# Block copies of the transposed norm and feed-forward blocks moved to SBUF-to-SBUF transfers, and x split for two tiles at once

## The chip, the cores and the metric

The kernel runs on one core of a Trainium2 chip. The metric is the device time of one execution in microseconds (us), the median of three runs. Engines: PE (TensorE, matmuls; PEld its weight loads), DVE (VectorE), ACT (ScalarE), POOL (GpSimd) and SP (SyncE, which here only issues DMAs). Each engine works through its own instructions in order.

## The reference

A trunk of two residual layers over 256 tokens of width 2048, all in float32. Layer 0 mixes tokens by grouped-query attention, layer 1 by a recurrent block (projection, convolution, two gated scans, output projection); each is followed by a SwiGLU feed-forward block of width 5632.

```python
for i in range(DEPTH):
    h = rms_norm(x, norm_mix[i])
    if i % N_MIXERS == 0:
        mix = attention_mixer(h, attn_w_qkv[j], ...)
    else:
        mix = recurrent_mixer(h, rnn_w_in[j], ...)
    x = x + mix
    x = x + swiglu(rms_norm(x, norm_ffn[i]), ffn_w_gate[i], ffn_w_up[i], ffn_w_down[i])

def rms_norm(x, g):
    y = xf * lax.rsqrt(jnp.mean(xf * xf, axis=-1, keepdims=True) + EPS)
    return y * g

def swiglu(h, w_gate, w_up, w_down):
    return (jax.nn.silu(h @ w_gate) * (h @ w_up)) @ w_down
```

## The kernel before

**Split matmuls.** Every matmul operand is a pair: hi, a rounded copy (made by ACT), and lo, the remainder (made by DVE as raw minus hi). A product is three matmuls: hi by hi, lo by hi, hi by lo. Weights stream from HBM in loads of 512 KB, issued by SP into eight buffers named raw (L140 in `load_half`, L157 in `load_seven`). `load_half` makes one cast (L145) and one remainder (L146) of a load. `load_seven` takes a pair of loads (gate and up) and makes the operands of a seven-product scheme: combinations of blocks on DVE (L169, the first of them by an accumulating DMA of POOL, L176, or on DVE, L174), casts L163 and L170 (its first is called ohi), remainders L164 and L171 (olo, lo). PE's order is the order of the code; the other engines' order is set by a scheduler from its own model of time, except where `follow` and `behind` chain instructions: `behind("cast", ...)` and `behind("rest", ...)` keep ACT's casts and DVE's remainders in the order of the code.

**x.** The residual stream `x_tm` lies with tokens on partitions (128 x 2 x 2048). A norm (class `Norm`) needs it with features on partitions. As soon as a group of 512 columns of x is final, `Norm.add(g)` squares it for the mean (L444) and calls `turn(g, engines)`: `turn_blocks` transposes 32 x 32 blocks in one DVE instruction (L408, tile two or x into one), and 16 copies of 32 partitions x 256 columns (L416, one into two) put the blocks where a 128-wide transpose would have them. The engines given in the call share the copies: ACT and POOL for groups 0 to 2, DVE, ACT and POOL for group 3. `scale` then makes the pair of each of the four tiles: ACT scales by the gain (L435), DVE takes the remainder (L436). For the feed-forward norm `form` makes four more operands per pair of tiles (ACT scale L466, four POOL instructions L472, cast L474, remainder L475: tiles form, fh, fl). The tiles one and two exist once each.

**Feed-forward units.** `ffn` runs 11 units of 512 hidden features per layer. In a unit, PE goes over eight pairs of tiles of x: those listed in SEVEN (or FEWER for the first three units) take 21 matmuls of 512 columns for two loads, the others 24. The unit's end combines the accumulators on DVE (L770 to L773, L791, L794, L795), with SiLU on ACT, into h (tile two). h is turned like x: one transpose, 16 copies, and then `whole` makes the split pair act (cast L801, remainder L802). Units 1 to 9 spread this over the next unit: the list `tail` holds four pieces of four copies each, the last one with `whole`, and every `load_seven` takes one piece. All copies of units 0 to 9 are ACT's; unit 0 does them in one piece at once, and unit 10 shares them between ACT and DVE. Between the units stand the down products, drained by ACT (L818) and added to x by accumulating DMAs of POOL.

**The recurrent layer's norm.** After the feed-forward block of layer 0 the norm of layer 1 is turned the same way, group 3 last. `Norm.spread` (L492, L493) makes the row of token factors: dg on DVE, and two small matmuls of PE that stand between those of the first projection.

Of the kernel before, what the change touches and what calls it, by code (L numbers as in the profile page):

```python
# [12 lines left out]
F32 = mybir.dt.float32  # L13
# [5 lines left out]
P = 128  # L19
# [55 lines left out]
def trunk(ctx, tc, w, out):  # L75
# [242 lines left out]
    def block(xs, k, a):  # L318
        return tuple(xs[k][:, s + a * P : s + (a + 1) * P] for s in (0, S))
# [85 lines left out]
    def turn_blocks(src, engines, own=None, spread=None):  # L405
        turned = tmp("one", (P, 2, WIDE), bufs=1)
        own = tmp("two", (P, 2, WIDE), bufs=1) if own is None else own
        dve.transpose(turned, src)  # L408
        t = own.rearrange("p a (b c) -> p (a b) c", c=S)

        def move(i):
            of = turned[32 * i : 32 * i + 32].rearrange("p a (k j c) -> p k a j c", k=4, j=4)
            for j in range(4):
                to = t[32 * j : 32 * j + 32].rearrange("p k (a i c) -> p k a i c", a=2, i=4)
                eng = engines[(4 * i + j) % len(engines)]
                m = (eng.copy if eng is act else eng.tensor_copy)(to[:, :, :, i, :], of[:, :, :, j, :])  # L416
                if spread is not None:
                    behind("cast", m)

        for i in range(4):  # L420
            move(i) if spread is None else spread.append(partial(move, i))
        return t

    class Norm:
# [5 lines left out]

        def scale(self, src):
            k = len(self.xs)
            g = col(self.g[0], self.g[1] + k)
            t = xp.tile([P, 2 * S], F32R, tag="xg", name=nm("xg"), bufs=16)
            newest["xh"] = act.activation(t[:, :S], src, AF.Copy, scale=g)  # L435
            newest["xl"] = dve.scalar_tensor_tensor(  # L436
                t[:, S:], src, g, t[:, :S].bitcast(F32), ALU.mult, ALU.subtract
            )
            self.xs.append(t)
# [6 lines left out]
        def add(self, g):  # L446
# [4 lines left out]
            self.turn(g, (act, pool) if g < NW - 1 else (dve, act, dve, pool))  # L451
# [3 lines left out]
        def turn(self, g, engines):  # L455
            t = turn_blocks(x_tm[:, :, g * WIDE : (g + 1) * WIDE], engines)
            for k in range(4):
                self.scale(t[:, k, :])
            for i in range(2):
                if self.g[0] == "norm_ffn" and 2 * g + i in SEVEN:  # L460
                    self.form(2 * g + i, t[:, 2 * i : 2 * i + 2, :])

        def form(self, c, src):
            v, t = (tmp("form", (P, 2 * S)).rearrange("p (a b) -> p a b", a=n) for n in (2, 4))
            for j in range(2):
                act.activation(v[:, j, :], src[:, j, :], AF.Copy, scale=col(self.g[0], self.g[1] + 2 * c + j))  # L466
# [283 lines left out]
    def ffn(norm, nxt):  # L750
# [3 lines left out]
        def unit(seven, beside, engines, soon):  # L754
# [42 lines left out]
            t, ht = act_four(), turn_blocks(h, engines, h, tail if beside else None)  # L797

            def whole(move=list):
                move()  # L800
                act.copy(t[:, :, :S], ht)  # L801
                dve.tensor_tensor(t[:, :, S:], ht, t[:, :, :S].bitcast(F32), ALU.subtract)  # L802

            if beside:
                tail.append(partial(whole, tail.pop()))
            else:
                whole()
            return [t[:, k, :] for k in range(UNIT)]
# [3 lines left out]
        for what, i in ffn_plan():  # L812
            if what == "unit":
                hid[int(np.searchsorted(ends, i, "right"))] += unit(FEWER.get(i, SEVEN), 0 < i < ends[-1] - 1, (act,) if i < ends[-1] - 1 else (act, dve), i < ends[0])
# [228 lines left out]
```

## Time and profile before

| | |
|---|---|
| median of 3 runs | 1953.04 us (1952.99 to 1953.76) |
| the profiled execution | 1952.89 us, span 1951.1 us |
| granted TensorE clock | 1.000 |
| PE busy | 1938.0 us of the span, 9224 matmuls |
| DVE, ACT, POOL busy | 1768.6, 1448.3, 401.3 us |
| DMA | 426 MB, q1 (SP) 58.0% and q0 (POOL) 11.9% of 16 engines' span |

How to read the rows: in the timeline a row is the start, the duration, the engine, the line, the operation, out<-in, the shape and the count; in brackets stands the idle time of the engine before it and who ended it. Matmuls are pipelined and a row's duration overlaps the next, so the distance between starts tells how fast PE goes. A row of a stretch has its length, each engine's busy time with the number of instructions, the granted clock, and the DMA share. A group's row has busy time and mean ns after the first bar, idle time before them after the second. A row of DMA issues ends with the median time from issue to landing.

### The profile page before, as it was taken

To read this page: it belongs to the slowest core of one execution; us is meant where nothing else is said; L and a number is where in the kernel's file an instruction comes from. 1 tells how busy PE (TensorE), PEld (TensorE's weight loads), DVE (VectorE), ACT (ScalarE), POOL (GpSimd) and SP (SyncE) were. 2 spreads that over 40 slices of the span, in tenths; PEclk is the share of its full clock that TensorE was granted. 3 is DMA by queue.
4 is the path that set the end of the run, shared out by engine and by line. 5 is a ranking of instruction groups with operands and counts; after the bars stand their busy time and mean duration, and the time that the engine had idled before them with its cause. 6 is when DMAs were issued, how large, how long until landed. Compare 5 with 4: busy or idle time off the path is not lost.

```text
span 1951.1 us, 27630 instructions
## 1 busy us (share of the span) xinstructions
PE 1938.0 (99%) x9224; PEld 1624.0 (83%) x9224; DVE 1768.6 (91%) x2417; ACT 1448.3 (74%) x2358; POOL 401.3 (21%) x497
## 2 busy tenths in 40 slices
PE   9999999999999999999999999999999999999999
PEld 8898888788888888888899998887888888888887
DVE  7878698999999999998799997898999999999993
ACT  7677686777777777777698887866778776787772
POOL 0442250011101111010465450520101111011100
PEclk9999999999999999999999999999999999999999
DMA  8434746698878978787365556555878888788872
GB/s 328 156 127 152 248 158 197 196 272 236 248 233 243 262 240 246 235 244 246 126 223 188 189 164 245 175 194 174 253 236 248 245 248 253 231 246 251 246 257 86
DMA packets 131727, 426.42 MB, mean 219 GB/s; under 512 B 14720, under 2 KB 14976, under 8 KB 131584
## 3 DMA queue, kind: packets, MB, share of 16 engines
q1 hardware_dynamic: 108944, 383.21, 58.0%
q0 software_dynamic: 22496, 41.43, 11.9%
q8 instruction: 72, 1.18, 0.2%
q14 instruction: 71, 0.58, 0.1%
q10 hardware_dynamic: 144, 0.02, 0.0%
HBM read 382.13 MB, written 2.10 MB: 197 GB/s over the span
## 4 chain that ended last, share of the span: by engine, by line
PE 92%; DVE 4%; ACT 1%; issue 1%; DMA 1%; POOL 0%; SPq 0%; ACTq 0%; DVEq 0%; POOLq 0%
PE acc L326 14%; PE acc L323 14%; PE acc L324 14%; PE pm L326 11%; PE pm L323 11%; PE pm L324 11%; PE acc L294 8%; PE acc L292 4%; PE pm L306 1%; PE pm L307 1%; PE pm L305 1%; DVE lo L146 1%; ACT hi L145 1%; DVE lo L164 0%; DMA raw<-in_w_in_dram 0%
## 5 line engine op out<-in xcount | busy, mean ns | idle before, releaser
L146 DVE TENSOR_TENSOR lo<-raw,hi 128x1024 fp32r<-128x1024 f32 (+1 forms) x474 | 574.5, 1240 | 77.1 <-ACT hi L145 75.3
L145 ACT CAST hi<-raw 128x1024 fp32r<-128x1024 f32 (+1 forms) x474 | 478.4, 1045 | 116.5 <-PE acc L324 72.1
L326 PE MATMUL acc<-lo,xg 128*128 128x512 f32 x744 | 290.9, 391 | 2.0 <-DVE lo L146 1.8
L323 PE MATMUL acc<-hi,xg 128*128 128x512 f32 x744 | 290.0, 390 | 0.0
L324 PE MATMUL acc<-hi,xg 128*128 128x512 f32 x744 | 289.6, 389 | 0.0
L164 DVE TENSOR_TENSOR lo<-raw,hi 128x1024 fp32r<-128x1024 f32 x232 | 275.0, 1217 | 6.5 <-ACT hi L163 3.8
L294 PE MATMUL acc<-xg,hi 128*128 128x512 f32 x832 | 271.7, 397 | 0.6 <-ACT hi L145 0.6
L163 ACT CAST hi<-raw 128x1024 fp32r<-128x1024 f32 x232 | 234.6, 1048 | 41.0 <-issue 14.4
L176 POOL DMA_DIRECT2D raw<-raw x90 | 77.7, 863 | 903.9 <-DVE raw L174 369.5
L323 PE MATMUL pm<-hi,act 128*128 128x512 f32 x512 | 199.2, 389 | 0.0
L324 PE MATMUL pm<-hi,act 128*128 128x512 f32 x512 | 199.2, 389 | 0.0
L326 PE MATMUL pm<-lo,act 128*128 128x512 f32 x512 | 199.2, 389 | 0.0
L416 ACT COPY two<-one 32x256 f32<-32x256 f32 x420 | 169.7, 404 | 24.7 <-DVE one L408 16.5
L292 PEld LDWEIGHTS acc<-xg,lo 128*128 128x128 f32 x832 | 156.3, 188 | 35.4 <-DVE lo L146 2.8
L323 PE MATMUL acc<-hi,act 128*128 128x512 f32 x448 | 174.9, 390 | 0.4 <-DVE two L794 0.4
L326 PE MATMUL acc<-lo,act 128*128 128x512 f32 x448 | 174.4, 389 | 0.0
L324 PE MATMUL acc<-hi,act 128*128 128x512 f32 x448 | 174.4, 389 | 0.0
L292 PE MATMUL acc<-xg,lo 128*128 128x256 f32 x832 | 171.8, 281 | 1.2 <-DVE lo L146 1.2
L326 PEld LDWEIGHTS acc<-lo,xg 128*128 128x128 f32 x744 | 139.7, 188 | 34.1 <-DVE lo L146 5.4
L324 PEld LDWEIGHTS acc<-hi,xg 128*128 128x128 f32 x744 | 139.7, 188 | 29.2
L323 PEld LDWEIGHTS acc<-hi,xg 128*128 128x128 f32 x744 | 139.7, 188 | 28.6
L170 ACT CAST hi<-raw 128x512 fp32r<-128x512 f32 x232 | 137.1, 622 | 32.8 <-DVE raw L169 31.8
(221 smaller groups left out, 3852.1 us busy)
## 6 DMA issues: line engine op xcount, KB each, us to landing
raw<-in_w_gate_dram SPq DMA_DIRECT2D x176, 512.0 KB, 4.6
raw<-in_w_up_dram SPq DMA_DIRECT2D x176, 512.0 KB, 5.5
raw<-in_w_down_dram SPq DMA_DIRECT2D x176, 512.0 KB, 4.4
raw<-in_w_in_dram SPq DMA_DIRECT2D x64, 512.0 KB, 4.4
raw<-raw POOLq DMA_DIRECT2D x90, 256.0 KB, 5.8
raw<-in_w_q_dram SPq DMA_DIRECT2D x32, 512.0 KB, 3.8
raw<-in_w_o_dram SPq DMA_DIRECT2D x32, 512.0 KB, 4.2
x<-form POOLq DMA_DIRECT2D x64, 256.0 KB, 6.7
```

The costliest lines, as they stand in the source:

```text
L145: behind("cast", act.copy(hi[:, sl], raw[:, sl]))
L146: behind("rest", dve.tensor_tensor(lo[:, sl], raw[:, sl], hi[:, sl].bitcast(F32), ALU.subtract))
L163: behind("cast", act.copy(hi, src))
L164: behind("rest", dve.tensor_tensor(lo, src, hi[:].bitcast(F32), ALU.subtract))
L170: behind("cast", act.copy(hi, o))
L176: pool.dma_start(out=t1, in_=b11, accum_op=ALU.add)
L292: pe.matmul(acc[:, S:], w, xs[k][:, :S], start=False, stop=stop)
L294: pe.matmul(acc, w, xs[k], start=(k == 0), stop=stop)
L323: pe.matmul(o, xh, wh, start=start, stop=False)
L324: pe.matmul(o, xl, wh, start=False, stop=False)
L326: pe.matmul(o, xh, wl, start=False, stop=stop)
L416: m = (eng.copy if eng is act else eng.tensor_copy)(to[:, :, :, i, :], of[:, :, :, j, :])
```

## The change

`turn_blocks` becomes `move_blocks`. The transpose is made in two halves (one per half of the tokens, 512 columns each, reading and writing in strides), so that each of the 16 moves is 32 partitions x 256 columns in one piece. If no engines are given, the 16 moves are DMAs from SBUF to SBUF issued by SP. This holds for all turns of the norms except group 3 of the recurrent layer's (still DVE, ACT and POOL), and for units 0 to 9 of each feed-forward block; unit 10 keeps ACT and DVE. Unit 0 now also defers `whole`; it stands behind the third `load_seven` of the next unit. `Norm.scaled` treats two tiles at once: two scales of ACT into v (tile form), one cast of both (xg, hi), one remainder of both on DVE; `form` takes v from it. The tiles xg and act hold their pairs in another layout, which `block` knows.

```diff
     def block(xs, k, a):
+        if isinstance(xs[k], tuple):
+            t, n = xs[k]
+            return tuple(t[:, s, a, n, :] for s in range(2))
         return tuple(xs[k][:, s + a * P : s + (a + 1) * P] for s in (0, S))
...
-    def turn_blocks(src, engines, own=None, spread=None):
+    def move_blocks(src, engines, own=None):
         turned = tmp("one", (P, 2, WIDE), bufs=1)
         own = tmp("two", (P, 2, WIDE), bufs=1) if own is None else own
-        dve.transpose(turned, src)
-        t = own.rearrange("p a (b c) -> p (a b) c", c=S)
-
-        def move(i):
-            of = turned[32 * i : 32 * i + 32].rearrange("p a (k j c) -> p k a j c", k=4, j=4)
+        one, two = (t.rearrange("p a b -> p (a b)") for t in (turned, own))
+        for a in range(2):
+            dve.transpose(
+                one.rearrange("p (j a e) -> p j a e", j=4, a=2)[:, :, a, :],
+                src[:, a, :].rearrange("p (k j c) -> p j k c", k=4, j=4),
+            )
+        for i in range(4):
             for j in range(4):
-                to = t[32 * j : 32 * j + 32].rearrange("p k (a i c) -> p k a i c", a=2, i=4)
-                eng = engines[(4 * i + j) % len(engines)]
-                m = (eng.copy if eng is act else eng.tensor_copy)(to[:, :, :, i, :], of[:, :, :, j, :])
-                if spread is not None:
-                    behind("cast", m)
-
-        for i in range(4):
-            move(i) if spread is None else spread.append(partial(move, i))
-        return t
+                to, of = two[32 * j : 32 * j + 32, S * i : S * i + S], one[32 * i : 32 * i + 32, S * j : S * j + S]
+                if engines is None:
+                    sync.dma_start(out=to, in_=of)
+                else:
+                    eng = engines[(4 * i + j) % len(engines)]
+                    (eng.copy if eng is act else eng.tensor_copy)(to, of)
+        return two
...
+        def scaled(self, src):
+            k = len(self.xs)
+            v = tmp("form", (P, 2 * S)).rearrange("p (a b) -> p a b", a=2)
+            for j in range(2):
+                to = v[:, j, :] if len(src.shape) == 3 else v[:, j, :].rearrange("p (a i c) -> p a i c", a=2, i=4)
+                act.activation(to, src[:, j], AF.Copy, scale=col(self.g[0], self.g[1] + k + j))
+            t = xp.tile([P, 2, 2 * S], F32R, tag="xg", name=nm("xg"), bufs=KT // 2)
+            hi, lo = t[:, :, :S], t[:, :, S:]
+            newest["xh"] = act.copy(hi, v)
+            newest["xl"] = dve.tensor_tensor(lo, v, hi.bitcast(F32), ALU.subtract)
+            self.xs += [t[:, j, :] for j in range(2)]
+            return v
...
-            self.turn(g, (act, pool) if g < NW - 1 else (dve, act, dve, pool))
+            self.turn(g, (dve, act, dve, pool) if g == NW - 1 and self.g[0] == "norm_mix" else None)
...
-            for k in range(4):
-                self.scale(t[:, k, :])
             for i in range(2):
+                v = self.scaled(t[:, 2 * i : 2 * i + 2])
                 if self.g[0] == "norm_ffn" and 2 * g + i in SEVEN:
-                    self.form(2 * g + i, t[:, 2 * i : 2 * i + 2, :])
+                    self.form(2 * g + i, v)
...
-            t, ht = act_four(), turn_blocks(h, engines, h, tail if beside else None)
+            t = act_four().rearrange("p k s -> p (k s)").rearrange("p (s q) -> p s q", s=2)
+            ht = move_blocks(h, engines, h).rearrange("p (i q c) -> p q i c", i=4, c=32)
...
-            if beside:
-                tail.append(partial(whole, tail.pop()))
+            if engines is None:
+                tail.extend([list, list, whole])
             else:
                 whole()
```

PE's instructions and their order stay the same, and up to the end of the attention layer nothing is moved on any engine. Three places of the order. First SP in a unit of the first feed-forward block. Before, the loads of the next unit (raw, from the gate and up weights) follow each other:

```order
L157 DMA raw_5127<-in_w_up_dram 128x1024
L140 DMA raw_5177<-in_w_gate_dram 128x1024
L140 DMA raw_5195<-in_w_up_dram 128x1024
L157 DMA raw_5213<-in_w_gate_dram 128x1024
L157 DMA raw_5214<-in_w_up_dram 128x1024
```

Now, printed with what each waits for (DMAHW0 to DMAHW7 are eight semaphores that SP's DMAs use in turn, so that each DMA waits for the one eight places ahead of it to land; the rows between the first two and the last of the 16 moves are alike):

```order
L140 DMA raw_5165<-in_w_gate_dram 128x1024 [waits DMAHW4_49,DVE_49]
L140 DMA raw_5183<-in_w_up_dram 128x1024 [waits DMAHW5_49,DVE_49]
L421 DMA two_4463<-one_4833 32x256 [waits DMAHW6_49,DVE_49]
L421 DMA two_4463<-one_4833 32x256 [waits DMAHW7_49]
...
L421 DMA two_4463<-one_4833 32x256 [waits DMAHW5_49]
L157 DMA raw_5201<-in_w_gate_dram 128x1024 [waits DMAHW6_49,DVE_49]
L157 DMA raw_5202<-in_w_up_dram 128x1024 [waits DMAHW7_49,DVE_49]
```

The 16 moves of the last unit's h stand between the loads of the next unit's wide pair and those of its fourth combined pair. Second, SP at the start of the first feed-forward block, around the moves of group 3 of its norm. Before:

```order
L140 DMA raw_3507<-in_w_gate_dram 128x1024
L140 DMA raw_3530<-in_w_up_dram 128x1024
L140 DMA raw_3586<-in_w_gate_dram 128x1024
L140 DMA raw_3604<-in_w_up_dram 128x1024
L140 DMA raw_3622<-in_w_gate_dram 128x1024
```

Now:

```order
L140 DMA raw_3508<-in_w_up_dram 128x1024
L140 DMA raw_3563<-in_w_gate_dram 128x1024
L140 DMA raw_3581<-in_w_up_dram 128x1024
L421 DMA two_3149<-one_3148 32x256 x16
L140 DMA raw_3599<-in_w_gate_dram 128x1024
```

The moves stand behind the first two loads of unit 1 (raw_3563 and raw_3581, in the profile before the loads at 276.71 and 278.11 us). Third, DVE at the end of the recurrent layer's norm (acc: the last products of group 3; xg_9201 to xg_9210 before, xg_9196 and xg_9202 now: group 2; xg_9358 to xg_9367 before, xg_9354 and xg_9360 now: group 3). Before:

```order
L436 SCALAR_TENSOR_TENSOR xg_9210<-two_9183,pk,xg_9210 128x256
L349 SCALAR_TENSOR_TENSOR x<-acc_9214,nr_3161,x 128x512
L408 STREAM_TRANSPOSE one_9339<-x 128x1024
L480 TENSOR_REDUCE nm_9329<-ssq_3211 128x2
L416 COPY two_9340<-one_9339 32x8x32 x2
L485 TENSOR_SCALAR nm_9329<-nm_9329 128x2
L416 COPY two_9340<-one_9339 32x8x32 x6
```

Now:

```order
L352 SCALAR_TENSOR_TENSOR x<-acc_9206,nr_3141,x 128x512
L413 STREAM_TRANSPOSE one_9331<-x 128x4x128 x2
L424 COPY two_9332<-one_9331 32x256 x8
L443 TENSOR_TENSOR xg_9196<-form_9193,xg_9196 128x2x256
L443 TENSOR_TENSOR xg_9202<-form_9199,xg_9202 128x2x256
L496 TENSOR_REDUCE nm_9321<-ssq_3189 128x2
L501 TENSOR_SCALAR nm_9321<-nm_9321 128x2
L443 TENSOR_TENSOR xg_9354<-form_9351,xg_9354 128x2x256
L519 TENSOR_TENSOR rsq_s_9325<-nm_9321,nr_9324 128x2
L443 TENSOR_TENSOR xg_9360<-form_9357,xg_9360 128x2x256
L146 TENSOR_TENSOR lo_9526<-raw_9524,hi_9525 128x1024
L508 TENSOR_SCALAR dg_9449<-ident,nr_9324 128x128 x2
```

Group 2's remainders, which stood ahead of group 3's transpose, now stand behind its copies, and dg, which stood directly behind the last xg and the three small instructions of the factor, now has a weight remainder (lo_9526) ahead of it.

More of the change, by code (lines that the diff above doesn't have):

```diff
@@ L433, in scale @@
             g = col(self.g[0], self.g[1] + k)
-            t = xp.tile([P, 2 * S], F32R, tag="xg", name=nm("xg"), bufs=16)
+            if k % 2 == 0:
+                self.pair = xp.tile([P, 2, 2 * S], F32R, tag="xg", name=nm("xg"), bufs=KT // 2)
+            t = self.pair[:, k % 2, :]
             newest["xh"] = act.activation(t[:, :S], src, AF.Copy, scale=g)
@@ L455, in turn, with form @@
         def turn(self, g, engines):
-            t = turn_blocks(x_tm[:, :, g * WIDE : (g + 1) * WIDE], engines)
-            for k in range(4):
-                self.scale(t[:, k, :])
+            t = move_blocks(x_tm[:, :, g * WIDE : (g + 1) * WIDE], engines)
+            t = t.rearrange("p (i a k c) -> p k a i c", i=4, a=2, k=4)
             for i in range(2):
+                v = self.scaled(t[:, 2 * i : 2 * i + 2])
                 if self.g[0] == "norm_ffn" and 2 * g + i in SEVEN:
-                    self.form(2 * g + i, t[:, 2 * i : 2 * i + 2, :])
[L463 to L466, printed above, removed]
+                    self.form(2 * g + i, v)
+        def form(self, c, v):
+            t = tmp("form", (P, 2 * S)).rearrange("p (a b) -> p a b", a=4)
             (a11, a21), (a12, a22) = ([v[:, j, a * P : (a + 1) * P] for a in range(2)] for j in range(2))
@@ L752, in bank, with unit @@
             return ps_m.tile([P, 2 * S], F32, tag="pm", name=nm("pm"))
-        def unit(seven, beside, engines, soon):
+        def unit(seven, engines, soon):
             xs, r = norm.xs, [norm.r[:, a : a + 1] for a in range(2)]
@@ L796, in unit, with whole @@
             ahead.extend([[1 if soon else 3, features, "rest"], [2 if soon else 4, last, "rest"]])
-            t, ht = act_four(), turn_blocks(h, engines, h, tail if beside else None)
[L799 to L802, printed above, removed]
-            if beside:
-                tail.append(partial(whole, tail.pop()))
+            t = act_four().rearrange("p k s -> p (k s)").rearrange("p (s q) -> p s q", s=2)
+            ht = move_blocks(h, engines, h).rearrange("p (i q c) -> p q i c", i=4, c=32)
+            def whole():
+                hi, lo = (t[:, s, :].rearrange("p (q i c) -> p q i c", i=4, c=32) for s in range(2))
+                behind("cast", act.copy(hi, ht))
+                behind("rest", dve.tensor_tensor(lo, ht, hi.bitcast(F32), ALU.subtract))
+            if engines is None:
+                tail.extend([list, list, whole])
             else:
                 whole()
-            return [t[:, k, :] for k in range(UNIT)]
+            blocks_of = t.rearrange("p s (a k c) -> p s a k c", a=2, k=UNIT)
+            return [(blocks_of, k) for k in range(UNIT)]
         hid = [[] for _ in PARTS]
@@ L813, in ffn @@
             if what == "unit":
-                hid[int(np.searchsorted(ends, i, "right"))] += unit(FEWER.get(i, SEVEN), 0 < i < ends[-1] - 1, (act,) if i < ends[-1] - 1 else (act, dve), i < ends[0])
+                hid[int(np.searchsorted(ends, i, "right"))] += unit(FEWER.get(i, SEVEN), None if i < ends[-1] - 1 else (act, dve), i < ends[0])
             else:
```

## The prediction

> **What bounds the kernel now.** I read the page's first part, then stretches of 26 us, then what PE waits for.
>
> ```profile
> PE 1938.0 (99%) x9224; PEld 1624.0 (83%) x9224; DVE 1768.6 (91%) x2417; ACT 1448.3 (74%) x2358; POOL 401.3 (21%) x497
> core 0: us, PE busy (x) PEld busy (x) DVE busy (x) ACT busy (x) POOL busy (x), PEclk, DMA share, GB/s
> 340.00:366.00 26.00, 23.84 (x99) 17.91 (x99) 25.34 (x33) 17.44 (x24) 0.00 (x0) 1.00 0.53 177
> 1337.00:1363.00 26.00, 23.80 (x99) 17.88 (x99) 25.34 (x33) 17.43 (x24) 0.00 (x0) 1.00 0.51 174
> 500.00:526.00 26.00, 26.00 (x116) 21.52 (x116) 25.52 (x32) 17.81 (x22) 0.00 (x0) 1.00 0.67 220
> PE pm L323 <- ACT ohi L170: 2.4, 2, 1.2
> PE acc L326 <- DVE lo L146: 1.8, 3, 0.8
> ```
>
> PE is the bound and the change leaves its instructions and their order alone, so whatever is freed on ACT, DVE and POOL is worth only PE time that is lost now. An undisturbed stretch (500 to 526) holds 116 matmuls, 0.224 us apart; the start of each feed-forward layer (340 and 1337) holds 99. Seventeen missing matmuls are 3.8 us; with one at the edges uncertain I take 3.7 us in each layer, 7.4 us in all. DVE is full in all three stretches (25.3 to 25.5 of 26 us). Where the 7.4 us is lost:
>
> ```profile
> 349.98 0.39 PE L324 MATMUL acc<-hi,xg 128*128 128x512 f32 x1
> 351.20 0.50 PE L326 MATMUL acc<-lo,xg 128*128 128x512 f32 x1 [0.84 <-DVE lo L146]
> 358.86 0.39 PE L326 MATMUL acc<-lo,fh 128*128 128x512 f32 x1
> 360.42 0.50 PE L323 MATMUL pm<-ohi,fh 128*128 128x512 f32 x1 [1.18 <-ACT ohi L170]
> 320.76 6.64 ACT L416 COPY two<-one 32x256 f32<-32x256 f32 x16 [1.11 <-DVE one L408]
> 328.08 0.69 DVE L171 TENSOR_TENSOR olo<-raw,ohi 128x512 fp32r<-128x512 f32 x1 [4.19 <-ACT ohi L170]
> 279.21 3.83 DVE L416 COPY two<-one 32x256 f32<-32x256 f32 x8
> 358.07 1.65 ACT L416 COPY two<-one 32x256 f32<-32x256 f32 x4 [3.37 <-DVE one L408]
> 359.75 0.62 ACT L170 CAST ohi<-raw 128x512 fp32r<-128x512 f32 x1
> ```
>
> The first PE wait is for a remainder on DVE. DVE is late because it spent 3.83 us on copies at 279 and stood idle 4.19 us at 328, behind the 16 copies that ACT makes in one piece. The second is for a cast that stands on ACT behind four copies. All these copies are of the kind that moves to SP.
>
> **The change part by part.** Durations, from the groups, and one row of the timeline for ACT's scales (four in 1.71 us, 0.45 each):
>
> ```profile
> L416 ACT COPY two<-one 32x256 f32<-32x256 f32 x420 | 169.7, 404 | 24.7 <-DVE one L408 16.5 <-DVE xg L436 2.2 <-DVE nm L480 0.6
> 948.07 1.71 ACT L435 ACTIVATE xg<-two,pk 128x256 fp32r<-128x256 f32 x4
> L436 DVE SCALAR_TENSOR_TENSOR xg<-two,pk,xg 128x256 fp32r<-128x256 f32 x48 | 21.2, 498 | 0.1
> L408 DVE STREAM_TRANSPOSE one<-two 128x1024 f32<-128x1024 f32 x22 | 27.1, 1233 | 0.0
> L171 DVE TENSOR_TENSOR lo<-raw,hi 128x512 fp32r<-128x512 f32 x232 | 150.1, 688 | 0.0
> ```
>
> *Removed.* Twenty of 22 units and 11 of 12 norm turns give up 16 copies each: 496 in all, 320 of them units' on ACT (320 x 0.404 = 129 us). Off PE's path nearly everywhere; on it only at the two layer starts. There DVE gains the eight copies' 3.8 us and the 4.2 us wait, 8 us where PE lacks 3.7, and the ohi cast no longer stands behind copies. So the stalls should go whole: -7.4 us. If the cover were half as large, half of them would stay.
>
> *Norm turns.* Four remainders of 0.498 become two of 512 columns at 0.688 (-0.6 us on DVE). ACT's four scales of 256 become four scales and two casts of 512 (0.62 each, as the ohi cast above); for the forms the separate scales disappear. Before 196 us nothing moves; the pairing of x there changes only tile names, 0 us.
>
> *Transposes.* One of 1024 columns becomes two of 512 with strided operands, which no row shows. Lower bound: half each, 2 x 0.62 = 1.23, no change. Upper: each as long as the whole, +1.23 us. I take 2 x 0.65, nearest to the 512-column rows, which cost little more than half of the 1024-column ones: +0.1 us a turn. It is hidden by the smallest lead of DVE over PE in a unit:
>
> ```profile
> 453.68 2.35 DVE L146 TENSOR_TENSOR lo<-raw,hi 128x1024 fp32r<-128x1024 f32 x2
> 455.63 0.39 PE L323 MATMUL pm<-hi,act 128*128 128x512 f32 x1
> ```
>
> The first of the two ends at 453.68 + 1.2 = 454.9 and PE takes it at 455.63: a lead of 0.7 us at each unit's end. +0.1 fits; a second microsecond would not.
>
> *The transfers.* 496 of 32 KB on SP's queue. By the order's waits each DMA on SP waits for the one eight places ahead to land, so a turn is two trips: the first eight pass once the last weight load ahead has landed, the other eight wait for the first eight. The trip's length no row has; bounds:
>
> ```profile
> out_dram<-x SPq DMA_DIRECT2D x8, 256.0 KB, 2.0
> raw<-raw POOLq DMA_DIRECT2D x90, 256.0 KB, 5.8
> raw<-in_w_up_dram SPq DMA_DIRECT2D x176, 512.0 KB, 5.5
> 464.66 0.33 SPq L140 DMA_DIRECT2D raw<-in_w_up_dram  x1
> 472.45 0.33 SPq L157 DMA_DIRECT2D raw<-in_w_gate_dram  x1
> 467.43 1.23 DVE L408 STREAM_TRANSPOSE one<-two 128x1024 f32<-128x1024 f32 x1
> 481.80 1.65 ACT L416 COPY two<-one 32x256 f32<-32x256 f32 x4
> ```
>
> I take the store's 2.0 us (SP's queue, and the weight loads have landed by then), up to 5.8 for the range. In a unit the last load leaves at 464.66 and lands about 5.5 later, at 470; the transposes end at 469; two trips of 2.0 and 16 issues of at most 0.33 end by 477. The cast that needs them stands behind the third combined load, where ACT now makes its third group of copies, at 481.8: 5 us to spare. SP's next load, at 472.45 before, goes about 3 us later, in a stretch where SP was waiting for a free buffer anyway: 0 us.
>
> The Trainium skill speaks against this form: "DMA: Bandwidth & Descriptors", section "Rules for kernel authors", says that two transfers to disjoint groups of partitions serialize and should be one, and that under 64 KB one pays mostly overhead; were the 16 wholly in series at 2.0 us each, a turn would take 32 us instead of 4 and the sum would fail (a rival below).
>
> *First feed-forward turn (group 3).* Its transfers stand behind two loads of unit 1:
>
> ```profile
> 278.11 0.33 SPq L140 DMA_DIRECT2D raw<-in_w_up_dram  x1
> 288.36 2.25 POOL L472 TENSOR_TENSOR form<-form 128x128 f32<-128x128 f32 x2 [5.48 <-ACT form L466]
> 290.69 1.73 POOL L472 TENSOR_TENSOR form<-form,form 128x128 f32<-128x128 f32 x2
> 299.03 0.39 PE L323 MATMUL pm<-hi,fh 128*128 128x512 f32 x1
> ```
>
> Last load ahead 278.1 + 5.5 = 283.6; two trips 287.6; scales 0.9, POOL's four 4.0, cast and remainder 1.3: 293.8. PE takes the form at 299.0: 5 us to spare with 2.0 us trips, 2.4 us late with 5.8.
>
> *The recurrent layer's norm.* Here the order costs something: group 2's remainders now stand behind group 3's transposes and copies on DVE, and one weight remainder ahead of dg.
>
> ```profile
> 950.00 1.26 DVE L436 SCALAR_TENSOR_TENSOR xg<-two,pk,xg 128x256 fp32r<-128x256 f32 x3
> 954.69 2.16 DVE L416 COPY two<-one 32x256 f32<-32x256 f32 x6
> 957.48 1.69 DVE L436 SCALAR_TENSOR_TENSOR xg<-two,pk,xg 128x256 fp32r<-128x256 f32 x4
> 959.20 0.48 DVE L492 TENSOR_SCALAR dg<-ident,nr 128x128 f32<-128x128 f32 x2
> 959.80 0.68 PE L493 MATMUL pm<-dg,ones 128*128 128x128 f32 x4 [0.73 <-DVE dg L492]
> 936.39 0.33 SPq L140 DMA_DIRECT2D raw<-in_w_in_dram  x1
> ```
>
> Now the copies end at 956.85. Without the four remainders ahead they end near 955.0; group 2's come at 955.0 to 956.3; PE wants them near 955.5, since 20 matmuls (ten of 512 columns at 0.224, ten of 256 at half that, 3.4 us) stand between them and L493's place near 958.9: +0.3 us. Group 3's scales and casts on ACT (copies, squares, four scales of 0.45, two casts of 0.6) let the second pair finish on DVE near 959.5; then a remainder of 1.2, then dg near 961.0 instead of 959.2. PE waits 1.7 to 2.4 there instead of 0.7 to 0.9. Together +1.3 us (0 to +3). The transfers of group 2 end at 936.4 + 4.4 + 2 x 2.0 = 944.8, before ACT's 948.07.
>
> *Sum.* -7.4 + 1.3 = -6.1. The profiled execution took 1952.89 us (span 1951.1 and 1.8 around it), 0.15 under the median of the runs. 1952.9 - 6.1 = **1946.8 us**. All the rest of the changed work lies beside PE.
>
> **The rivals.**
> A, the slow trip. At POOL's 5.8 us a trip the forms come at 283.6 + 11.6 + 6.2 = 301.4, 2.4 us late in each layer (+4.8); group 2 of the recurrent norm lands at 952.4, 4.3 us behind ACT's place for it (+4.3); in a unit the turn ends between 481.6 and 484.2 against 481.8, of which 0.7 is covered, so 0 to 1.7 us in 20 units (I take 0.3, +6). 1946.8 + 15 = 1962, slower. It decides from about 5.4 us a trip; from 3.6 the recurrent norm pays, from 4.5 the forms. For it: the weights' traffic; against: that has landed when the second eight go. 15%.
> B, half of it stays. DVE's chain at the layer start waits for the late group-3 turn (DVE's remainder of it stands between a combined load's instructions), so only half of the 7.4 us returns: 1952.9 - 3.7 + 1.3 = 1950.5, no difference. 17%.
> C, the strided transposes take the whole's time: +1.2 us on DVE in 20 units, of which 0.7 is covered: 20 x 0.5 = 10 us; 1946.8 + 10 = 1957, slower. Against: the rows scale with columns. 8%.
> D, the transfers run one after another: 32 us a turn, against 13 between transpose (469) and use (482): 19 us on ACT in 20 units, hundreds of us; 2100 or more. Against it: transfers overlap now, since one load of 512 KB at a time in 5.5 us would be 95 GB/s, and the stretch from 500 shows 220. 2%. By the rule of the Trainium skill named above it would follow if serializing meant whole trips; no row here shows that.
>
> **How the numbers follow.** Forecast 58%, B 17%, A 15%, C 8%, D 2%. 0.2% (3.9 us) is about what a measurement of this kernel can tell from no change: faster means under 1949.1, slower over 1956.9. Faster: 56 of the forecast's 58 and 4 of B's: 0.60. Slower: 8 of A's, C and D: 0.18. Same: 0.22. The range runs from 1944.0 (the recurrent norm costs nothing, and another microsecond and a half is won at units' ends) to 1957.0, where B and half of A are in; left out are C, D, half of A and the tail below: 2 in 10. The forecast's own range is 1944 to 1949.
>
> **What would show it.** Right: 114 to 116 matmuls in the two stretches, no ohi wait of PE; ACT near 1290 us busy; transposes of 0.65 us; the 32 KB transfers landing in 2 to 2.5 us; dg's wait on PE grown to about 2 us. Wrong: PE waiting for forms or ACT idle at the scales for transfers (A, B); transposes of 1.2 us and remainders late at each unit's end (C).

## The result: 5% slower, and the profile after

The changed kernel takes 2052.68 us (median, 2045.36 to 2053.31) against 1953.01 for the kernel before on the same chip: ratio 1.0502, 95% interval 1.0478 to 1.0526. The prediction said 1946.8 and a range up to 1957.0; the time lies 96 us above the range. Its profiled execution has a span of 2051.3 us, 100.2 more than before. First the page: the engines' busy time, the chain that ended last, and the transfers (count, KB each, median us from issue to landing).

```profile
PE 1987.6 (97%) x9224; PEld 1623.3 (79%) x9224; DVE 1757.8 (86%) x2411; ACT 1293.3 (63%) x1958; POOL 353.8 (17%) x417
PE 50%; DVE 22%; DMA 9%; SPq 9%; issue 6%; ACT 3%; POOL 1%; DVEq 0%; ACTq 0%; POOLq 0%
two<-one SPq DMA_DIRECT2D x496, 32.0 KB, 2.6
```

ACT lost its copies, as forecast (1290 expected, 1293.3 measured), and of the engines only PE is busy for longer: the same 9224 matmuls fill 1987.6 us instead of 1938.0, at a mean granted clock of 0.988 instead of 1.000. New is SP's queue in the chain, with 9%. What the transfers cost that queue stands in the line's own answer (duration in ns, least/median/most) and in a steady unit's timeline, before and after:

```profile
L421 SPq DMA_DIRECT2D two<-one x496: 507/589/1805, 226.2 to 1931.8; - x166
```

```profile
528.63 1.24 DVE L408 STREAM_TRANSPOSE one<-two 128x1024 f32<-128x1024 f32 x1
533.66 0.33 SPq L157 DMA_DIRECT2D raw<-in_w_gate_dram  x1
```

```profile
547.88 1.30 DVE L413 STREAM_TRANSPOSE one<-two 128x512 f32<-128x512 f32 x2
549.21 13.37 SPq L421 DMA_DIRECT2D two<-one  x16
562.67 0.53 SPq L157 DMA_DIRECT2D raw<-in_w_gate_dram  x1
564.08 1.05 ACT L818 CAST act<-two 128x1024 fp32r<-128x1024 f32 x1 [2.75 <-DMA two<-one]
```

Before, SP's next weight load leaves 3.8 us after the transpose ends (529.87 to 533.66); now 13.5 us after it (549.18 to 562.67), since SP issues the 16 moves first. So the loads that stand behind the moves go late. And the cast of the turned tile, which needs the last move, waits for it: the turn is late too. Over the other steady units the delay of the load is 12.4 to 13.8 us. Who waits for what, from the waits (total us, times, longest); of before only one row, for comparison:

```profile
PE acc L326 <- ACT hi L145: 17.7, 2, 8.8
PE pm L329 <- DVE olo L171: 17.7, 36, 0.5
ACT hi L163 <- DMA raw<-raw: 62.2, 16, 9.2
DVE lo L164 <- ACT hi L163: 61.5, 21, 9.0
ACT act L818 <- DMA two<-one: 35.3, 16, 3.7
DVE act L819 <- ACT act L818: 37.2, 19, 3.7
ACT form L439 <- DMA two<-one: 31.6, 10, 6.8
DVE one L413 <- DMA two<-one: 20.4, 7, 5.2
```

```profile
ACT hi L163 <- DMA raw<-raw: 1.8, 2, 0.9
```

Two chains lead to DVE, which had 0.5 us to spare in 26. A late load makes ACT's cast L163 late, and with it DVE's remainder L164. A late turn makes the cast act late, and with it DVE's remainder of act. The third new wait, of DVE's transposes (one L413), is the norms': tile one exists once, and a group's transposes have to wait until the transfers of the group before have read it.

Since PE's order is the same in both kernels, the n-th matmul of one can be set against the n-th of the other. The table gives how many us each profiled execution lies behind the kernel before at that place; the experiments' columns are used below.

```
place (us in before)              after units_act norms_eng end_free half poolq half_dummy half_fixed engines before_unit0
 280 before group 3's form          0.0   -0.3       0.5      0.7     0.1  -0.2    0.0       -0.3      -0.2    -0.5
 325 group 3's form used            5.1    3.7       1.0      4.3     4.0   3.9    4.0        0.2       0.3    -0.5
 374 first units of ffn 0           3.3    3.5      -0.8      2.5     3.0   2.7    2.9       -0.8      -0.8    -1.6
 398                               12.7    5.2       8.7     11.4     5.4   3.7   10.8        1.6       1.0    -1.6
 874 steady units done             35.0   13.0      34.1     31.4     6.2  24.0   41.4        2.2       1.0    -1.6
 897 unit 10 and its end           48.6   25.3      46.7     34.0    17.6  35.8   54.2        3.0       1.2    -1.6
 962 recurrent norm                55.9   32.9      49.6     41.4    25.3  43.2   61.6        5.9       2.5    -1.6
1302 recurrent layer done          55.7   33.5      48.9     43.1    25.1  42.8   60.9        5.4       3.6    -1.3
1374 first units of ffn 1          54.8   35.5      47.2     41.3    25.3  41.6   60.9        5.5       2.5    -2.4
1397                               63.3   35.9      56.4     50.1    25.3  42.5   66.9        5.1       3.9    -2.6
1873 steady units done             87.7   42.4      78.6     74.2    25.9  62.0  101.7        5.3       3.9    -2.6
1896 unit 10 and its end          100.3   55.1      90.8     76.5    37.6  75.0  114.7        5.3       4.1    -2.6
```

So the first column loses 5.1 us at the first forms, wins 1.8 back at the layer start, loses 31.8 and 32.9 in the units of the two layers, 13.5 and 12.6 at the layers' ends, and 7.3 in the recurrent norm.

The two ends are a surprise of another kind. PE stands still behind a weight cast of the down matrix. ACT's rows there, after and then before, and PE's after:

```profile
921.78 1.28 ACT L535 ACT_TABLE_LOAD   x1
924.39 3.29 ACT L424 COPY two<-one 32x256 f32<-32x256 f32 x8 [1.33 <-DVE one L413]
927.72 1.04 ACT L818 CAST act<-two 128x1024 fp32r<-128x1024 f32 x1
928.67 4.83 ACT L145 CAST hi<-raw 128x1024 fp32r<-128x1024 f32 x5
```

```profile
886.40 1.28 ACT L519 ACT_TABLE_LOAD   x1
887.70 1.05 ACT L145 CAST hi<-raw 128x1024 fp32r<-128x1024 f32 x1
890.04 1.06 ACT L145 CAST hi<-raw 128x1024 fp32r<-128x1024 f32 x1 [1.28 <-issue]
892.71 1.06 ACT L145 CAST hi<-raw 128x1024 fp32r<-128x1024 f32 x1 [1.62 <-PE acc L324]
895.43 1.06 ACT L145 CAST hi<-raw 128x1024 fp32r<-128x1024 f32 x1 [1.66 <-PE acc L324]
896.49 3.31 ACT L416 COPY two<-one 32x256 f32<-32x256 f32 x8
```

```profile
929.76 0.80 PE L326 MATMUL acc<-hi,act 128*128 128x512 f32 x1 [8.85 <-ACT hi L145]
```

Before, four weight casts stand between the table load and unit 10's eight copies on ACT; now none does. Unit 10 isn't turned by SP at all. But the new `whole` enters its cast and remainder with `behind`, for every unit, in the rows that fix the order of weight casts and remainders; before, these two were in no row. Recorded before the down matrix's loads, they now come first.

### The profile page after: what moved, and what is told of

It is laid out like the page before. It is cut to its first block, busy times and chain, and to the rows that moved or that the text cites. A ratio compares the mean times of both kernels' runs of the same rounds, so it can differ in the third digit from the quotient of the medians.

```text
span 2051.3 us, 27926 instructions
## 1 busy us (share of the span) xinstructions
PE 1987.6 (97%) x9224; PEld 1623.3 (79%) x9224; DVE 1757.8 (86%) x2411; ACT 1293.3 (63%) x1958; POOL 353.8 (17%) x417
## 4 chain that ended last, share of the span: by engine, by line
PE 50%; DVE 22%; DMA 9%; SPq 9%; issue 6%; ACT 3%; POOL 1%; DVEq 0%; ACTq 0%; POOLq 0%
SPq L421 9%; PE acc L329 8%; PE acc L294 8%; PE acc L326 8%; PE acc L327 8%; DVE lo L164 5%; DVE lo L146 5%; DMA raw<-raw 4%; PE acc L292 4%; DVE raw L169 4%; PE pm L329 4%; PE pm L326 3%; PE pm L327 3%; DMA raw<-in_w_up_dram 2%; DVE olo L171 2%
## 5 line engine op out<-in xcount | busy, mean ns | idle before, releaser
L164 DVE TENSOR_TENSOR lo<-raw,hi 128x1024 fp32r<-128x1024 f32 x232 | 277.3, 1220 | 63.7 <-ACT hi L163 61.5
L163 ACT CAST hi<-raw 128x1024 fp32r<-128x1024 f32 x232 | 236.5, 1048 | 113.5 <-DMA raw<-raw 62.2
L170 ACT CAST ohi<-raw 128x512 fp32r<-128x512 f32 x116 | 71.9, 620 | 226.7 <-DVE raw L169 220.4
L169 DVE TENSOR_TENSOR raw<-raw,raw 128x512 f32<-128x512 f32 x232 | 150.6, 690 | 3.8
```

Of the source, the lines that this page charges most:

```text
L163: behind("cast", act.copy(hi, src))
L164: behind("rest", dve.tensor_tensor(lo, src, hi[:].bitcast(F32), ALU.subtract))
L169: behind("rest", dve.tensor_tensor(o, x, y, op))
```

## The experiments

Three theories of the loss: Q, the moves hold SP's queue; O, unit 10's place in the order; S, the strided transposes and the merged casts and remainders are slow themselves.

**units_act.** The units' moves on ACT again, in three pieces.

```diff
-                if engines is None:
+                if spread is not None:
+                    spread.append(partial(lambda t, o: behind("cast", act.copy(t, o)), to, of))
+                elif engines is None:
                     sync.dma_start(out=to, in_=of)
...
-                tail.extend([list, list, whole])
...
+                tail.extend([partial(some, n) for n in (0, 6, 12)])   # six copies; the last with whole
```

> The changed kernel, but the 16 block moves of each of units 0 to 9 are ACT copies (six, six and four behind the first three combined loads); the norms' turns stay transfers. Matched matmul by matmul, the changed kernel loses 31.8 + 4.5 us in the units of the first feed-forward layer and 32.9 + 3.5 in those of the second. Theory Q (SP's queue: a move holds it for 0.63 us, a turn for 10 to 14 us, so the turn lands late and the weight loads behind it go late): these 72.7 us vanish, 2052.7 - 72.7 = 1980, with the 9 us at each layer's end, the forms (4.6) and the recurrent norm (7.3) left. Rival S (the strided transposes and the merged casts and remainders, which stay, are what costs): 2040 to 2053.

Measured: 2007.35 us, ratio 1.0278 (1.0261 to 1.0295): 45.3 us less, between the two expectations. By the table the units of a layer still lose 7 to 10 us, evenly, some 1 us each. The waits point to the reason: with six copies ahead of ACT's cast DVE waits for it, which it hardly did before (2.8 us in 16 waits of at most 0.2). So this run mixes the removal of the transfers with a new crowding on ACT, and the run half, below, has to decide.

```profile
DVE act L822 <- ACT act L821: 31.2, 22, 2.0
```

**norms_eng.** One line back:

```diff
-            self.turn(g, (dve, act, dve, pool) if g == NW - 1 and self.g[0] == "norm_mix" else None)
+            self.turn(g, (act, pool) if g < NW - 1 else (dve, act, dve, pool))
```

> The changed kernel, but the norms' turns are copies on ACT and POOL (DVE, ACT and POOL for the last group) again; the units' moves stay transfers. Theory Q: the late forms (4.6 us at 297 to 303, 0.9 at 1361) and the wait of 5 us for group 2 at 1004 go, some 11 us: 2042. Rival S: the pairs of scales, casts and remainders are themselves late: within 3 us of the changed kernel.

Measured: 2045.27 us, ratio 1.0477 (1.0461 to 1.0492): 7.4 us less, not 11. By the table it loses 0.5 us at the first forms where the changed kernel loses 5.1, so 4.6 of these come from the transfers. In the recurrent norm 2.9 us stay of 7.3. The edit is one line, but there it changed DVE's order as well, which the scheduler sets: with no transfers to wait for, group 2's remainders stand ahead of the copies again, and dg right behind the last remainder of group 3, with no weight remainder between. PE's wait of 4.8 us for group 2's remainders is gone, and another of 1.6, for a remainder of group 3, has come. So the run doesn't split the 7.3 us between the transfers and the order that the prediction costed.

**end_free.** Unit 10's two instructions out of the rows.

```diff
-                behind("cast", act.copy(hi, ht))
-                behind("rest", dve.tensor_tensor(lo, ht, hi.bitcast(F32), ALU.subtract))
+                c = act.copy(hi, ht)
+                r = dve.tensor_tensor(lo, ht, hi.bitcast(F32), ALU.subtract)
+                if engines is None:
+                    behind("cast", c)
+                    behind("rest", r)
```

> The changed kernel, but the cast and the remainder of unit 10 are not entered in the rows of weight casts and remainders, so that the down matrix's casts need not stand behind them. Theory O (order): PE's two waits of 9.0 us (920.5 and 1969.9) go, 2052.7 - 18 = 2035. Rival Q2 (the casts are late because the loads are): under 3 us, since the down matrix's loads then would still be the last to come.

Measured: 2031.45 us, ratio 1.04 (1.0385 to 1.0416): 21.2 us less. The steps at the layers' ends are 2.6 and 2.3 us instead of 13.5 and 12.6. Theory O holds, and each of the two waits cost more than its 9 us (last section).

**double.** Each move as two of half the columns.

```diff
-                    sync.dma_start(out=to, in_=of)
+                    for z in (0, S // 2):
+                        sync.dma_start(out=to[:, z : z + S // 2], in_=of[:, z : z + S // 2])
```

> The changed kernel with each move as two transfers of half the columns (32 of 16 KB a turn, the same bytes). Theory Q: the price is per transfer; a turn holds SP for 20 us instead of 10 and 20 units lose about 10 us more each, less what is covered: 2150 to 2260. Rival B (bytes: the transfers take bandwidth from the loads): within 10 us of 2053.

Measured, one run: 2347.56 us, 294.9 more than the changed kernel for 496 transfers more, 0.594 us each. One issue holds SP 0.589 us, and halving the bytes did not shorten that:

```profile
L422 SPq DMA_DIRECT2D two<-one x992: 507/589/1860, 223.6 to 2228.0; - x199
```

The price of an issue is per transfer, not per byte. That the time grew by just one issue per transfer is partly chance: the granted clock in this run was 0.936 against 0.988, so some of the 295 us is PE running slower behind longer waits. The expected range had counted on some cover and had no term for that.

**half.** Eight of a unit's 16 moves by SP, eight as ACT copies, four behind each of the first two combined loads.

```diff
+                if spread is not None and i > 1:
+                    spread.append(partial(lambda t, o: behind("cast", act.copy(t, o)), to, of))
-                if engines is None:
+                elif engines is None:
                     sync.dma_start(out=to, in_=of)
...
-                tail.extend([list, list, whole])
...
+                tail.extend([partial(some, 0), partial(some, 4), whole])   # four copies each
```

> The changed kernel, but of the 16 moves of each of units 0 to 9 only eight are transfers by SP; the other eight are ACT copies, four behind each of the first two combined loads. Theory Q (SP's queue, 0.63 us a move): a turn holds SP for 5 us instead of 10 to 14, lands before ACT's place for it, and the next loads go 5 us late instead of 10; the lead covers most of that, so the loss in the units (31.8 and 32.9 us in the two layers) falls to some 10 each: 2005 to 2015. Rival L (any transfer of this kind in the unit upsets the order of loads): half of the loss stays, 2020 to 2025.

Measured: 1990.4 us, ratio 1.0185 (1.0169 to 1.0201): 62.3 us less, more than either theory gave. In the steady units it loses 0.8 and 0.6 us a layer (5.4 to 6.2, 25.3 to 25.9), with the strided transposes and merged remainders in place; so S falls for the units. SP's rows:

```profile
535.70 1.30 DVE L413 STREAM_TRANSPOSE one<-two 128x512 f32<-128x512 f32 x2
537.03 6.78 SPq L423 DMA_DIRECT2D two<-one  x8
543.91 0.53 SPq L157 DMA_DIRECT2D raw<-in_w_gate_dram  x1
```

The next load leaves 6.9 us after the transposes end, 3 us later than before the change, and that is covered; the changed kernel's 10 us later is not. But in half the turn also ends sooner, so two causes are still joined: the loads that stand behind the moves, and the cast that waits for them.

**units_poolq.** The units' moves on POOL's queue, to free SP's loads of them.

```diff
-                    sync.dma_start(out=to, in_=of)
+                    (sync if own_tmp else pool).dma_start(out=to, in_=of)   # own_tmp: a norm's turn
```

> The changed kernel, but the units' moves are issued by POOL's queue instead of SP's, so that SP's weight loads stand behind none of them. A POOL issue took 0.86 us here, so a turn is issued in 14 us instead of 10 and lands 3 to 4 us later. Theory late loads (the loss comes from the weight loads that stand behind the moves on SP): most of the units' 65 us goes, about 1995. Theory late turn (ACT waits at the cast of the turned tile for the last move): 3 to 4 us more in each of 20 units, 2110 to 2130, more if POOL's exchanges for the next unit come late as well.

Measured: 2029.85 us, ratio 1.0397 (1.0382 to 1.0411): 22.8 us less, neither expectation. Such a transfer holds POOL 0.50 us, not the 0.86 that I took from its exchanges, yet the exchanges and accumulations on that queue now stand between and behind the moves. Two rows of a unit, and DVE's waits:

```profile
541.15 3.17 POOL L422 DMA_DIRECT2D two<-one  x5
553.57 1.54 POOL L176 DMA_DIRECT2D raw<-raw  x1
DVE act L820 <- ACT act L819: 55.0, 16, 4.8
DVE act L820 <- DMA x<-form: 17.3, 4, 4.5
DVE lo L164 <- ACT hi L163: 7.2, 6, 1.7
```

A third of the units' loss went (64.7 to 41.7 us by the table), and the waits tell where the rest is lost. SP's next load leaves 3.8 us after the transposes in all steady units, as before the change, and DVE hardly waits at L164 any more; but it waits 72 us for the turned tile, whose cast starts 16.2 us after the transposes end in this unit (14.9 in the unit of the changed kernel above). So a late turn costs time without any late load of SP. How late POOL's own exchanges came, this run can't tell, since ACT reaches their casts late itself.

**half_dummy.** The other way round: late loads without a late turn. Half, plus eight small transfers by SP, seven of them behind its eight moves and one ahead, into a tile that nothing reads.

```diff
                 if spread is not None and i > 1:
+                    if j == 0 and i == 2:
+                        dump = tmp("dump", (P, S), bufs=1)
+                    sync.dma_start(out=dump[32 * j : 32 * j + 32, P * (i - 2) : P * (i - 1)], in_=of[:, :P])
                     spread.append(...)
```

> The kernel of the run half (eight moves of a unit by SP, eight by ACT), plus eight further transfers by SP behind them in each of units 0 to 9, of 32x128 each into a tile that nothing reads. So SP is held, and the next weight loads stand behind 16 transfers, as in the changed kernel, while the moves that ACT waits for are the first eight. The changed kernel took 62.7 us more than half. Theory late loads: all of that comes back, 2040 to 2053. Theory late turn: it stays at half's 1990, within 5 us.

Measured: 2068.96 us, ratio 1.0598 (1.0583 to 1.0612): all of the 62.3 us is back, and 16 more. Its rows of a unit and of the waits:

```profile
549.28 7.04 SPq L426 DMA_DIRECT2D two<-one  x8
556.37 5.78 SPq L423 DMA_DIRECT2D dump<-one  x7
562.25 0.53 SPq L157 DMA_DIRECT2D raw<-in_w_gate_dram  x1
```

```profile
ACT hi L163 <- DMA raw<-raw: 112.5, 18, 8.8
PE pm L329 <- DVE olo L171: 23.9, 47, 0.5
```

No cast of a turned tile waits for a transfer here, and the loss is whole: late loads alone are enough. The combined load's data come late to POOL's exchange, its landing (raw<-raw) late to ACT's cast L163, that to DVE's remainders, and DVE, which has 0.5 us to spare in 26, makes PE wait at olo unit after unit. SP's next load leaves no later than in the changed kernel (11.6 to 13.1 us after the transposes in the steady units), so it isn't a still later load that makes this run 16 us worse. Set side by side, the runs show what the loss goes with:

| run | DVE idle at L164, for the load (us) | DVE idle at act, for the turn (us) | PE's loss in the units of both layers (us) |
|---|---|---|---|
| before | 3.8 | 2.8 | 0 |
| half | 18.5 | 4.0 | 3.7 |
| units_poolq | 7.2 | 72.3 | 41.7 |
| after | 61.5 | 37.2 | 64.7 |
| half_dummy | 106.2 | 4.0 | 79.2 |

The loss grows with DVE's idle time, whichever of the two makes it. In the changed kernel both do, one after the other in a unit, and the 16 issues on SP make both; the two runs that are without one of them still lose 41.7 and 79.2 us. Why the idle time at L164 is so much longer in half_dummy was not taken apart.

**half_fixed.** Half, with the edits of norms_eng and end_free.

> The kernel of the run half, with the norms' moves on the engines as before the change and unit 10's cast and remainder outside the rows of casts: the three causes taken away together. If they make up the whole loss, half's 37.5 us over the kernel before shrink by the two steps of 11.5 us at the layers' ends and by 8 to 11 us of the norms: 1953 to 1960. If a cause is missing: above 1965.

Measured: 1956.53 us, ratio 1.0021 (1.0011 to 1.003). The three causes (the units' moves, the norms' moves and unit 10's place) together are the loss up to 3.8 us.

**engines.** The changed kernel with all moves on engines (units 1 to 9 four copies behind each of four combined loads, unit 0 six, six and four), and the edits of norms_eng and end_free.

> The changed kernel with every move made by an engine again: units 1 to 9 by ACT, four behind each of four combined loads as before the change; unit 0 six, six and four behind three; norms as before; unit 10's cast and remainder not in the rows of casts. What is left of the change are the two strided transposes, the pairs of scales, casts and remainders, and unit 0's turn in pieces. Theory (the transfers and unit 10's place are the whole loss): 1945 to 1955. Rival S (strided transposes and pairs cost too): 1960 to 1975.

Measured: 1956.87 us, ratio 1.002 (1.0011 to 1.0029), 2 us above the first expectation and short of the second. No steady unit loses anything in its column; what is left stands in the first units of each layer (1.8 and 1.4 us), in the recurrent norm (1.3) and in the recurrent layer (1.1). The 1.3 equals the forecast by chance: DVE's order in that norm is the one described under norms_eng and not the one that was costed. No version with the merged pairs beat the kernel before.

**before_unit0.** The kernel before; only unit 0's copies on ACT come in three pieces.

```diff
+            if first:
+                a, b = tail.pop(0), tail.pop(0)
+                tail.insert(0, lambda: (a(), b()))
...
-unit(FEWER.get(i, SEVEN), 0 < i < ends[-1] - 1, (act,) if i < ends[-1] - 1 else (act, dve), i < ends[0])
+unit(FEWER.get(i, SEVEN), i < ends[-1] - 1, (act,) if i < ends[-1] - 1 else (act, dve), i < ends[0], i == 0)
```

> The kernel before, with one edit: unit 0's 16 copies on ACT stand behind three combined loads (eight, four, four) instead of in one piece. The prediction's reading (PE's stalls of 3.7 us at the start of each feed-forward layer come from unit 0's copies in one piece, with DVE idle 4.2 us behind them): half to all of 7.4 us goes, 1945.6 to 1949.5. Rival (DVE's copies at 279 and the sheer load of DVE cause them): 1952 to 1954.

Measured: 1950.35 us against 1952.92, ratio 0.9988 (0.9979 to 0.9997): 2.6 us faster, the only version whose interval lies below the kernel before, and about a third of the 7.4 us: between the two expectations. In the first of the stretches that the prediction rested on, and in the waits:

```profile
340.00:366.00 26.00, 24.43 (x104) 18.94 (x103) 23.64 (x29) 14.35 (x20) 0.00 (x0) 1.00 0.52 173
PE pm L323 <- ACT ohi L170: 2.5, 2, 1.3
```

104 matmuls instead of 99 (in the second layer's stretch too): five of the seventeen missing ones. The wait for the ohi cast stays whole.

**before_units01.** On top of that, unit 1's first four copies move from the first to the second combined load, out of that cast's way.

```diff
-            if first:
+            if first or second:
                 a, b = tail.pop(0), tail.pop(0)
                 tail.insert(0, lambda: (a(), b()))
+            if second:
+                tail.insert(0, list)
```

> The kernel of the run before_unit0, and unit 1's copies on ACT stand behind the second to fourth combined load (eight, four, four) instead of four behind each, so that the cast that PE waited 1.4 us for in each layer (357 and 1353) no longer stands behind four copies. The prediction's reading (that cast is late because of the copies in front of it): another 2 to 2.8 us, 1947.6 to 1948.5. Rival (the cast waits for DVE anyway, or the eight copies then delay the next one): 1950 to 1951.

Measured: 1951.78 us, ratio 0.9997 (0.9988 to 1.0006): no further gain. The wait for ohi is gone, and PE waits for DVE's olo a little later instead:

```profile
340.00:366.00 26.00, 25.24 (x108) 19.62 (x107) 24.25 (x30) 13.42 (x17) 0.00 (x0) 1.00 0.54 182
PE pm L326 <- DVE olo L171: 1.4, 3, 0.5
```

Its profiled execution also lost 2 us in the recurrent layer, which the edit doesn't touch; whether that is the edit's doing stays open.

## Why the prediction was wrong, step by step

- **The transfers: the step that failed.** The prediction gave a turn two trips of 2.0 us "and 16 issues of at most 0.33", over 8 us after the transposes. Measured, an issue holds SP 0.59 us and the next follows 0.63 us after it; 16 take 10 us, 13.4 in the steady unit above, where some issues held SP for up to 1.5 us, and the last lands 14.6 us after the transposes. So the term that failed is the price of an issue, 0.33 us where it is 0.63 from one to the next, and with it the 5 us to spare. The 0.33 was taken from loads of another shape and used as an upper end, while the trace had a dearer issue row, POOL's exchange at 0.86 us; 16 of these are 13.8 us. The bound from above was put on the trip alone, and the trip was not what decided: a transfer landed 1.7 us after its issue at the least and 2.6 in the median. The sums are also short by their own terms. In the unit, two trips and 16 issues from 470 end at 479.3, not 477. At group 3's form and in the recurrent norm the 16 issues (5.3 us) are left out altogether; with them the form comes at 299.1, just when PE takes it, and group 2 lands at 950.1, after ACT's 948.07.
- **SP's next load, costed at nothing.** The prediction had it about 3 us late "in a stretch where SP was waiting for a free buffer anyway". It comes 10 us late. Together with the late turn that is 62 us of the loss (half against the changed kernel), and half_dummy shows that the late loads alone are enough for it. Half shows that 3 us would indeed have been free: the mechanism was named with its cover, and the size was off by a factor of three.
- **Rival A** had the right sign and one of the two waits, ACT's for the landing (35.3 us), by another cause: not a trip of 5.8 us, but 16 issues. It missed the loads queued behind. Rival D, one after another, was nearer than its 2%: not the transfers, but their issues stand in series. Where several were queued behind a load, they landed 0.16 us apart (290.90, 291.05, 291.21, 291.37), so the transport itself wasn't the limit there. The Trainium skill's rule in "DMA: Bandwidth & Descriptors", section "Rules for kernel authors", that small transfers pay mostly overhead, agrees with the run double (an issue held SP 0.589 us at 32 KB and at 16 KB). Its rule on serializing warned against the right form, but it speaks of the transfers themselves; what stood in series here were the issues, 0.63 us apart.
- **Unit 10: a step left out.** The prediction has no term for it: `behind` in `whole` was never followed for the unit that is not deferred. It costs two waits of 9 us and, with what follows them, 21 to 23 us.
- **Group 3's form.** 5 us to spare were claimed; PE lost 5.1 us there, 4.6 of them to the transfers (norms_eng). Their turn took 14.9 us of SP instead of two trips of 2.0:

```profile
281.46 14.89 SPq L421 DMA_DIRECT2D two<-one  x16
299.36 0.50 PE L326 MATMUL pm<-hi,xg 128*128 128x512 f32 x1 [1.49 <-ACT xg L442]
```

  The third to the eighth of its moves went out one by one, each within 0.03 us of the landing of a weight load (283.22, 284.48, ... 290.75), the load eight places ahead whose semaphore it takes over: six loads had still to land one after the other, the last at 290.75, where the prediction let the last one land at 283.6. The other eight took 5.6 us more.
- **The recurrent norm.** +1.3 forecast, 7.3 measured, by a wait that the prediction did not have:

```profile
991.32 10.60 SPq L421 DMA_DIRECT2D two<-one  x16
1003.58 1.30 DVE L413 STREAM_TRANSPOSE one<-x 128x512 f32<-128x512 f32 x2 [4.22 <-DMA two<-one]
1008.93 0.79 PE L294 MATMUL acc<-xg,hi 128*128 128x512 f32 x1 [4.79 <-DVE xg L443]
```

  Group 2's moves hold SP for 10.6 us. Group 3's transposes write the tile one that these moves read, so they wait 4.2 us for the last of them. Group 2's remainders stand behind these transposes and the copies, by the very order that was costed at 0.3 us, and PE waits 4.8 us for them; the clock stands at 0.50 from 1008 to 1014 behind that wait. The wait for dg, forecast at 1.7 to 2.4 us, is 0.5. Without the transfers the norm loses 1.3 to 2.9 us, but in another order of DVE (norms_eng), so what the costed order alone would take stays open.
- **The layer starts.** -7.4 forecast; by the table the changed kernel wins 1.8 and 0.9 us there before it loses more, and before_unit0 2.6 in all. The stalls were put down to unit 0's copies and the ohi cast's place; with both mended (before_units01), DVE, full in that stretch, hands PE the next wait. Rival B's size (half or more stays) was right here; its reason, a late turn of group 3, is not what holds in before_units01, where that turn is as before.
- **Right:** the strided transposes (0.65 forecast, 0.685 measured), ACT's busy time, and that merged casts and remainders are free in the units.

Added up: half takes 62.3 of the 99.7 us between the medians away, half_fixed another 33.9, and 3.8 are left. Measured one by one on the changed kernel, unit 10's place (21.2) and the norms' moves (7.4) make 28.6 of these 33.9; the other 5 are not assigned (the runs of norms_eng alone spread from 2043.4 to 2049.7).

## What to carry to other kernels

Before work is moved to a queue of transfers, multiply the number of transfers by the dearest issue row that the trace has, and ask what stands behind them in that queue: here eight of 32 KB were free within the slack of the next weight loads, and sixteen, with the turn and the loads behind them late, cost 3 us of PE per unit. Count that row in every place where the transfers are issued, also where only the trip seems to matter. An instruction that is entered in an ordering rule must be followed for every caller, also the one that seems unchanged. On a kernel whose second engine is as full as its first, taking away a wait mostly shows the next one.

## What the runs showed of the hardware

A wait of PE can cost more than its length. In the run half, around unit 10's end of the first layer (granted TensorE clock in the column after POOL's):

```profile
894.00:895.00 1.00, 0.00 (x0) 0.00 (x0) 0.96 (x4) 0.98 (x3) 0.00 (x0) 0.70 0.00 0
895.00:896.00 1.00, 0.00 (x0) 0.00 (x0) 0.94 (x5) 0.96 (x4) 0.00 (x0) 0.50 0.00 0
903.00:905.00 2.00, 2.00 (x7) 1.58 (x6) 2.00 (x2) 1.99 (x3) 0.00 (x0) 0.59 0.93 260
905.00:907.00 2.00, 2.00 (x11) 1.62 (x10) 2.00 (x3) 0.91 (x1) 0.00 (x0) 1.00 0.97 350
```

PE stops at 890.4 and starts again at 899.2; its clock is at half from 894.4 to 904.6, so the 9.0 us of waiting became a step of 11.4. The short waits of before, at most 1.2 us, left it at 1.00. A wait between them may do either: the same run has a wait of 1.7 us in each feed-forward layer, and the clock stood at 0.50 from 1382.5 to 1385.8 behind the second and stayed at 1.00 behind the first. The Trainium skill, "TensorE: Matmul & The Clock Gate", section "Part 1: The HAM clock gate (the "warmup" mystery)", gives a window of about 3.4 us for both directions; the drop 4.0 us after the stop and the return 5.4 us after the start agree with a free-running window of that size. That a wait of half its length was once followed by half clock, it does not say; here the measurement counts.

Also not expected: a transfer from SBUF to SBUF of 32 partitions holds SP's queue 0.59 us, against 0.33 for a weight load of 16 times its bytes, and POOL's queue 0.50, against 0.86 for its accumulating exchange. What sets these was not tried.
